# A transformer block on one core: banks for the last head pair's values, and which weight parts are made beside the attention

## The chip, the core and the metric

The kernel runs on one core of a Trainium2 chip. It uses TensorE (matrix products; PE in the profile), VectorE (DVE), ScalarE (ACT), GpSimd (POOL) and the DMA queue of SyncE (SP). The metric is the device time of one execution in microseconds (us). The times before are 2073.45, 2076.32 and 2074.26 us; their median is 2074.26 us.

## What is computed

The input x is 512 rows of 2048 numbers, all in 32-bit floats:

```python
h = rmsnorm(x, g_attn);  proj = h @ w_in            # 2048 x 6152
oa = stick_breaking_attention(8 heads);  ob = forgetting_attention(8 heads)
x = x + concat(headnorm(oa), headnorm(ob)) @ w_out  # 2048 x 2048
u = relu(rmsnorm(x, g_mlp) @ w_up);  x = x + (u * u) @ w_down
y = rmsnorm(x, g_final)
```

Every operand of a product is split into a high part (the value cast to TensorE's rounded 32-bit type) and a low part (what the cast lost), and each product is three matmuls: high by high, high by low, low by high.

## The kernel before, in words

There are four stages: the projections together with the attention, the output projection, the up projection, the down projection. This case is about the end of the first and the start of the second.

**Projections and attention.** The 16 heads are taken in eight pairs (`for n in range(0, 2 * NH, 2)`), the forgetting heads first, stick-breaking heads 6 and 7 last. For each pair `project_q` makes queries and keys of both heads (four products, `accq` in the profile), and `accumulate_v` makes the values of two pairs at a time, or, for the last pair, of that pair alone (`accv`). The weights come in 512 KB pieces through three buffers (tag `wraw`), are split by ScalarE (`wh`) and VectorE (`wl`) into three pairs of buffers (tags `wh`, `wl`), and are multiplied. `take_v` scales and splits the values (`vh` on ScalarE, `vl` on VectorE). `attend` computes the scores (`s`), turns them into weights (`w`), transposes these (`pt`), splits them (`ph`, `pl`) and multiplies them with the values (`o`; for the last head `oq`). Then the head is normalized by its mean square (the matmuls with `onesr`, lines 273 and 274) and written to `mixed`.

Sums of `accq` and `accv` are kept in four PSUM banks of one pool, `acc`, taken in turn. `s`, `pt` and `oq` share three further banks, `o` and `ssq` one.

**Weight sums beside the attention.** `sums_of_weights(m)`, called for m = 0 to 7 during the first four pairs, loads 2 MB of `w_out`, forms the sums and differences of its four blocks which the output projection needs, and writes them to DRAM (`wsums`). It also writes some operands as ready high and low parts: for product 1 both parts (`wfirst`, made in the tile `tfirst`), for products 5 and 6 the high part (`whigh`, from the tile `thi`), the low part replacing the sum itself in `wsums`. `tfirst` and `thi` take turns in one buffer, so each waits until the one before has been written out.

**Output projection.** It works by seven block products instead of eight (Winograd's form), in the order 1, 2, 6, 5, 7, 3, 4, for two halves of columns (`db`). Each product has four pieces (`out_piece(p, db, m0)`, m0 = 4, 6, 0, 2) of 12 matmuls. A piece takes its weights in one of two ways: as ready parts, two loads of 512 KB straight into a high and a low buffer; or raw, one load of 512 KB into a `wraw` buffer (named `wo`), with the split on ScalarE and VectorE. For db = 0 the products 1, 5 and 6 go by parts, 2, 7, 3 and 4 raw. The places for high and low parts are handed out in turn by `hi_lo`: three buffers, and a fourth (`wx`, in the pool `px`) as long as `more_parts` holds it, which for db = 0 begins with product 6 and ends after product 5.

The sums of products 1, 6, 7 and 4 are kept in A (`accoa`), of 2 in B (`accob`), of 5 and 3 in C (`accoc`), for db = 0. A and B, two banks each, lie where the four `acc` banks lay; C lies in the banks of the scores. The other operands are forms of `mixed` (`g_form`: a sum of blocks where needed, then a split into `G[p]`); those of product p for m0 = 2 need heads 6 and 7 and come last. After a product `take` adds its bank to a quarter of x; a finished quarter is transposed (`tr`), written to DRAM (`xd`) and, once that write has landed, squared in place (line 686).

**What sets the order.** The kernel is written with a tile layer. Its planner places the instructions on each engine's queue by its own estimates; `tc.high_priority()` and `tc.issue_after(...)` steer it. On the chip each queue runs in the order that was planned, and an instruction that waits holds up all that stand behind it on its queue. SyncE's queue is in order too: a load that waits for its buffer holds up the loads behind it.

Of the kernel before, what the change touches and what calls it, by code (L numbers as in the profile page):

```python
# [14 lines left out]
P = 128  # L15
# [20 lines left out]
def block_kernel(ctx, tc, x, g_attn, w_in, b_f, g_out_sb, g_out_fox, w_out, g_mlp, w_up, w_down, g_final, y):  # L36
# [16 lines left out]
    up_cm = tc.tile_pool(name="u", bufs=1, side="right", reuse_waits="tile")  # L53
    up = up_cm.__enter__()
    dp = ctx.enter_context(tc.tile_pool(name="dp", bufs=1, space=bass.MemoryType.DRAM))
    acc_cm = tc.tile_pool(name="acc", bufs=4, space=PSUM, reuse_waits="tile")
    acc = acc_cm.__enter__()

    lows, last_heads = [None], [None] * 5

# [83 lines left out]


    wsums = dp.tile([P, NH // 2, 4, 2, 2, NT], F32, name="wsums")
    whigh = dp.tile([P, NH // 2, 2, 2, NT], F32, name="whigh")

    wfirst = dp.tile([P, NH // 2, 2, 2, NT], F32, name="wfirst")


    A_ORDER = (1, 4, 5, 6, 2, 7, 3)
# [5 lines left out]
    with tc.tile_pool(name="att", bufs=1, side="right", reuse_waits="tile") as at:  # L158
# [15 lines left out]
        def accumulate_v(c0, m, steps, prepare=None, more=None):  # L174

            per = NT // m
            banks = [acc.tile([P, NT], F32, tag="acc", name="accv") for _ in range(2 if more is not None else TB // per)]
# [142 lines left out]
        def v_columns(h):  # L320
            return 2 * WSB + h * P if h < NH else o0 + 2 * WSB + (h - NH) * P
# [64 lines left out]
        with tc.tile_pool(name="attp", bufs=1, space=PSUM, reuse_waits="tile") as atp:  # L386

            fl = at.tile([P, TB, NH], F32, name="fl")

            chl = at.tile([P, TB, P], F32, name="chl")  # L390
            pool.memset(chl, 0.0)
            cr = at.tile([P, TB, NH], F32R, name="cr")
            cq = at.tile([P, TB, NH], F32, name="cq")
            lf = at.tile([P, TB, 2 * NH], F32R, name="lf")
            fe = at.tile([P, TB, NH], F32, name="fe")
            for t in range(TB):
                dve.scalar_tensor_tensor(fl[:, t, :], ps[t][:, 2 * P:], r1[:, t:t + 1], bf, op0=ALU.mult, op1=ALU.add)
# [12 lines left out]
            dve.tensor_tensor(cq, cq, cps[:, :, NH:], op=ALU.add)  # L410
            act.copy(cr, cq)
            dve.tensor_copy(chl[:, :, :NH], cr.bitcast(F32))
            dve.tensor_tensor(chl[:, :, NH:2 * NH], cq, cr.bitcast(F32), op=ALU.subtract)
            cT = atp.tile([P, NT], F32, tag="o", name="cT")
            for t in range(TB):
                pe.transpose(cT[:, t * P:(t + 1) * P], chl[:, t, :], ident)
            ckT = at.tile([P, NT], F32R, name="ckT")
            act.copy(ckT, cT)

            def sums_of_weights(m):  # L420

                b = mixed[:, :NH].rearrange("p (q a) n -> p q (a n)", a=2)
                sp.dma_start(b.rearrange("p (s j) c -> p s j c", s=2),
                             w_out[2 * m * P:2 * (m + 1) * P].rearrange("(s p) (j c) -> p s j c", s=2, j=2))
                b11, b12, b21, b22 = (b[:, i] for i in range(4))
                first = at.tile([P, 2, NT], F32R, tag="thi", name="tfirst")
                split(first[:, 0], first[:, 1], b11[:, :NT])
                sp.dma_start(wfirst[:, m // 2, :, m % 2], first.bitcast(F32))
                dve.tensor_tensor(b11, b12, b11, op=ALU.subtract)
                dve.tensor_tensor(b12, b22, b12, op=ALU.subtract)  # L430
                dve.tensor_tensor(b22, b22, b11, op=ALU.subtract)
                dve.tensor_tensor(b21, b21, b22, op=ALU.subtract)
                t12 = b[:, ::3, :NT]
                hi = at.tile([P, 2, NT], F32R, tag="thi", name="thi")
                act.copy(hi, t12)
                dve.tensor_tensor(t12.bitcast(F32R), t12, hi.bitcast(F32), op=ALU.subtract)
                sp.dma_start(whigh[:, m // 2, :, m % 2], hi.bitcast(F32))
                sp.dma_start(wsums[:, m // 2, :, :, m % 2], b.rearrange("p q (d c) -> p q d c", d=2))

            for n in range(0, 2 * NH, 2):  # L440
                def project(i):
                    h = order[n + i]
                    e = (o0 if h >= NH else 0) + h % NH * P
                    return project_q(e, 2 * i, rbq), project_q(e + WSB, 2 * i + 1, rb)

                def attend(i, qk):
                    h = order[n + i]
                    with tc.high_priority():
                        (attend_fox if h >= NH else attend_sb)(h % NH, v, i, *qk)

                qk = [project(0), project(1)]
                if n < NH:
                    sums_of_weights(n)
                    sums_of_weights(n + 1)

                if n == 2 * NH - 2:
                    ps = accumulate_v([v_columns(order[n])], 2 * P, [4] * 4)
                    with tc.high_priority():
                        vs = take_v(ps)
                elif n % 4 == 2:  # L460
                    c = [v_columns(order[n + i]) for i in (0, 2)]
# [6 lines left out]
    acc_cm.__exit__(None, None, None)  # L468

# [145 lines left out]
    def out_piece(p, db, m0):  # L615

        hi, lo = (w.rearrange("p (a b) -> p a b", a=2) for w in hi_lo(2 * NT))
        if db == 0 and p == 1:
            begun_ = [sp.dma_start(w.bitcast(F32), wfirst[:, m0 // 2, i]) for i, w in enumerate((hi, lo))][1]
        elif db == 0 and p in (5, 6):  # L620
            begun_ = sp.dma_start(hi.bitcast(F32), whigh[:, m0 // 2, p - 5])
            sp.dma_start(lo.bitcast(F32), wsums[:, m0 // 2, 3 * (p - 5), db])
# [70 lines left out]
    for db in range(2):  # L693
        if db == 1:
            begin(0, 0, db)
        else:
# [3 lines left out]
            with tc.issue_after(last_heads[2].ins):  # L700
                for p in (4, 5):
                    g_form(p, (4, 8), (0, 2), (2, 3))
            out_piece(1, 0, 4)
            with tc.issue_after(last_heads[3].ins):
                out_piece(1, 0, 6)
# [411 lines left out]
```

## Time and profile before

| | |
|---|---|
| median of three runs | 2074.26 us |
| profiled execution, its own time | 2072.58 us |
| span of the profile | 2070.8 us |
| TensorE busy | 2050.2 us, 99% |
| VectorE busy | 1612.9 us, 78% |
| ScalarE busy | 1049.7 us, 51% |
| moved by DMA | 400.49 MB, 193 GB/s on average |

The profile is of one execution. A row of the timeline gives the start in us from the span's start, the duration, engine, line of the kernel before, operation, output and inputs, how many equal ones were merged and, in brackets, how long the engine was idle before it and what ended that. Matmuls overlap: of a row of matmuls it is the distance from start to start that counts, not the duration. A row of stretches gives the busy time of each engine in the stretch, then the TensorE clock, the share of time in which the DMA engines were busy, and GB/s.

### The profile page before, as it was taken

What the parts mean: (1) busy time and instruction counts of PE and PEld (TensorE: products, weight loads), DVE (VectorE), ACT (ScalarE), POOL (GpSimd) and SP (SyncE); (2) the same over time, 40 slices, a digit from 0 to 9 for tenths busy, and PEclk for the clock granted to TensorE, in tenths of its full rate; (3) what the DMA queues carried; (4) which work ended last, traced back from release to release, by engine and by line L of the source; (5) the groups of instructions that cost most, each with busy time, mean ns of one, the idle gap of its engine ahead of it and who ended that gap; (6) DMA issues with size and microseconds to landing.
All of it is one profiled execution on the core that took longest, in us unless ns stands there. A gap on an engine that the chain in (4) does not pass through costs nothing.

```text
span 2070.8 us, 29864 instructions
## 1 busy us (share of the span) xinstructions
PE 2050.2 (99%) x12000; PEld 1822.9 (88%) x12000; DVE 1612.9 (78%) x1764; ACT 1049.7 (51%) x1420; POOL 55.1 (3%) x76
## 2 busy tenths in 40 slices
PE   9999999999999999999999999999999999999998
PEld 8888888888897889999999999999888888888886
DVE  6767754657568478888888888888789888989895
ACT  6434433444455466656656665665743343433434
POOL 0000000000000000000000000000000000000003
PEclk9999999999999999999999999999999999999999
DMA  7878732323336872665665666567855664763722
GB/s 252 289 273 288 240 91 73 82 81 84 79 114 245 287 264 98 204 194 178 208 197 184 204 212 193 177 211 248 296 198 214 255 238 160 281 236 140 273 93 102
DMA packets 258218, 400.49 MB, mean 193 GB/s; under 512 B 9328, under 2 KB 154784, under 8 KB 250528
## 3 DMA queue, kind: packets, MB, share of 16 engines
q1 hardware_dynamic: 257120, 396.46, 57.1%
q8 instruction: 94, 1.54, 0.3%
q10 hardware_dynamic: 960, 2.13, 0.3%
q14 instruction: 44, 0.36, 0.1%
HBM read 307.85 MB, written 90.70 MB: 192 GB/s over the span
## 4 chain that ended last, share of the span: by engine, by line
PE 94%; DVE 3%; DMA 1%; issue 1%; ACT 1%; SPq 0%; ACTq 0%
PE accd L96 7%; PE accd L97 7%; PE accd L98 7%; PE psa L97 6%; PE psa L98 6%; PE psa L96 6%; PE accq L96 6%; PE accq L98 6%; PE accq L97 6%; PE psc L98 3%; PE psc L97 3%; PE psc L96 3%; PE accv L96 3%; PE accv L97 3%; PE accv L98 3%; PE psb L96 1%
## 5 line engine op out<-in xcount | busy, mean ns | idle before, releaser
L63 ACT CAST wh<-wu 128x1024 fp32r<-128x1024 f32 x171 | 178.3, 1048 | 136.4 <-PE psa L97 57.1
L64 DVE TENSOR_TENSOR wl<-wu,wh 128x1024 fp32r<-128x1024 f32 x171 | 208.1, 1221 | 45.8 <-ACT wh L63 44.9
L98 PE MATMUL psa<-f,wl 128*128 128x256 f32 x792 | 224.2, 283 | 0.3 <-DVE wl L64 0.3
L97 PE MATMUL psa<-f,wh 128*128 128x256 f32 x792 | 224.2, 283 | 0.1
L96 PE MATMUL psa<-f,wh 128*128 128x256 f32 x792 | 224.1, 283 | 0.0
L63 ACT CAST wh<-wd 128x1024 fp32r<-128x1024 f32 (+1 forms) x135 | 133.2, 996 | 173.2 <-PE accd L98 104.5
L96 PE MATMUL accq<-hH,wh 128*128 128x512 f32 x512 | 200.5, 392 | 0.1
L98 PE MATMUL accq<-hH,wl 128*128 128x512 f32 x512 | 200.4, 391 | 0.0
L97 PE MATMUL accq<-hL,wh 128*128 128x512 f32 x512 | 200.3, 391 | 0.0
L64 DVE TENSOR_TENSOR wl<-wd,wh 128x1024 fp32r<-128x1024 f32 (+1 forms) x135 | 153.7, 1149 | 35.4 <-ACT wh L63 35.0
L63 ACT CAST wh<-wraw 128x1024 fp32r<-128x1024 f32 (+2 forms) x101 | 101.9, 1010 | 153.1 <-PE accq L97 92.9
L98 PE MATMUL accd<-wh,uf 128*128 128x512 f32 x432 | 168.1, 389 | 0.0
L97 PE MATMUL accd<-wl,uf 128*128 128x512 f32 x432 | 168.1, 389 | 0.0
L96 PE MATMUL accd<-wh,uf 128*128 128x512 f32 x432 | 167.9, 389 | 0.0
L64 DVE TENSOR_TENSOR wl<-wraw,wh 128x1024 fp32r<-128x1024 f32 (+2 forms) x101 | 119.3, 1183 | 56.3 <-ACT wh L63 49.9
L63 ACT CAST wx<-wd 128x1024 fp32r<-128x1024 f32 (+1 forms) x89 | 89.2, 1005 | 125.9 <-PE accd L98 72.1
L98 PEld LDWEIGHTS psa<-f,wl 128*128 128x128 f32 x792 | 152.0, 192 | 0.5 <-DVE wl L64 0.5
L97 PEld LDWEIGHTS psa<-f,wh 128*128 128x128 f32 x792 | 152.0, 192 | 0.4 <-DVE f L64 0.3
L96 PEld LDWEIGHTS psa<-f,wh 128*128 128x128 f32 x792 | 152.0, 192 | 0.1
L64 DVE TENSOR_TENSOR wx<-wd,wx 128x1024 fp32r<-128x1024 f32 (+1 forms) x89 | 102.6, 1161 | 23.9 <-ACT wx L63 23.7
L96 PEld LDWEIGHTS accq<-hH,wh 128*128 128x128 f32 x512 | 96.2, 188 | 19.7 <-PE accv L98 0.5
L98 PEld LDWEIGHTS accq<-hH,wl 128*128 128x128 f32 x512 | 96.1, 188 | 19.5
(338 smaller groups left out, 5558.2 us busy)
## 6 DMA issues: line engine op xcount, KB each, us to landing
wu<-in_w_up_dram SPq DMA_DIRECT2D x60, 1024.0 KB, 6.9
ufd<-st SPq DMA_DIRECT2D x98, 512.0 KB, 7.0
wd<-in_w_down_dram SPq DMA_DIRECT2D x48, 1024.0 KB, 6.3
wraw<-in_w_in_dram SPq DMA_DIRECT2D x84, 512.0 KB, 3.9
uf<-ufd SPq DMA_DIRECT2D x42, 1024.0 KB, 6.8
mixed<-in_w_out_dram SPq DMA_DIRECT2D x8, 2048.0 KB, 8.3
wsums<-mixed SPq DMA_DIRECT2D x8, 2048.0 KB, 8.1
wo<-wsums SPq DMA_DIRECT2D x24, 512.0 KB, 5.3
```

The source lines that it names most:

```text
L63: ins = act.copy(hi, src)
L64: lows[0] = dve.tensor_tensor(lo, src, hi.bitcast(F32), op=ALU.subtract)
L96: pe.matmul(out, sh, mh, start=first, stop=False, skip_group_check=True)
L97: pe.matmul(out, sh, ml, start=False, stop=False, skip_group_check=True)
L98: return pe.matmul(out, sl, mh, start=False, stop=last, skip_group_check=True)
```

## The change

1. The pool `acc` becomes two pools of two banks, `accs[0]` and `accs[1]`, taken by turns; they lie where A and B will lie. The values of the last pair are taken from `accs[1]` alone, that is, from B's two banks.
2. `sums_of_weights` writes both parts for products 1 and 2 (`wraws`, two splits of 512 columns through the tile `tboth`) and the high part for product 6 alone (512 columns). Before it was both parts for product 1, and the high parts for 5 and 6 (one cast and one difference of 1024 columns). Per call it makes three small writes (512, 512 and 256 KB) beside `wsums`; before, two (512 and 512 KB).
3. For db = 0, product 2 goes by parts, and product 5 raw.
4. The fourth place for parts, `wx`, is there from product 1 on, not from product 6.
5. `take_squares` is tied to the last cast of output weights only where there has been one.

```diff
-    acc_cm = tc.tile_pool(name="acc", bufs=4, space=PSUM, reuse_waits="tile")
-    acc = acc_cm.__enter__()
+    acc_cms = [tc.tile_pool(name=f"acc{c}", bufs=2, space=PSUM, reuse_waits="tile") for c in "ab"]
+    accs = [cm.__enter__() for cm in acc_cms]
+    acc_turn = [0]
+    class acc:
+        @staticmethod
+        def tile(*args, **kwargs):
+            acc_turn[0] += 1
+            return accs[1 - acc_turn[0] % 2].tile(*args, **kwargs)
...
-                first = at.tile([P, 2, NT], F32R, tag="thi", name="tfirst")
-                split(first[:, 0], first[:, 1], b11[:, :NT])
-                sp.dma_start(wfirst[:, m // 2, :, m % 2], first.bitcast(F32))
+                for w, raw in zip(wraws, (b11, b21)):
+                    both = at.tile([P, 2, NT], F32R, tag="thi", name="tboth")
+                    split(both[:, 0], both[:, 1], raw[:, :NT])
+                    sp.dma_start(w[:, m // 2, :, m % 2], both.bitcast(F32))
...
-                t12 = b[:, ::3, :NT]
-                hi = at.tile([P, 2, NT], F32R, tag="thi", name="thi")
-                act.copy(hi, t12)
+                t2 = b22[:, :NT]
+                hi = at.tile([P, 2, NT], F32R, tag="thi", name="thi")[:, 0]
+                act.copy(hi, t2)
...
-                    ps = accumulate_v([v_columns(order[n])], 2 * P, [4] * 4)
+                    ps = accumulate_v([v_columns(order[n])], 2 * P, [4] * 4, pool_=accs[1])
...
-        if db == 0 and p == 1:
-            begun_ = [sp.dma_start(w.bitcast(F32), wfirst[:, m0 // 2, i]) for i, w in enumerate((hi, lo))][1]
-        elif db == 0 and p in (5, 6):
+        if db == 0 and p in (1, 2):
+            begun_ = [sp.dma_start(w.bitcast(F32), wraws[p - 1][:, m0 // 2, i]) for i, w in enumerate((hi, lo))][1]
+        elif db == 0 and p == 6:
...
+            more_parts.append(lambda: parts_at(px, "px"))
             out_piece(1, 0, 4)
...
-            if db == 0 and p == 6:
-                more_parts.append(lambda: parts_at(px, "px"))
...
-                with tc.issue_after(casts[0].ins):
+                with ExitStack() as order_:
+                    if casts[0] is not None:
+                        order_.enter_context(tc.issue_after(casts[0].ins))
                     take_squares()
```

More of the change, by code (lines that the diff above doesn't have):

```diff
@@ L146, in block_kernel @@
     wsums = dp.tile([P, NH // 2, 4, 2, 2, NT], F32, name="wsums")
-    whigh = dp.tile([P, NH // 2, 2, 2, NT], F32, name="whigh")
-    wfirst = dp.tile([P, NH // 2, 2, 2, NT], F32, name="wfirst")
+    whigh = dp.tile([P, NH // 2, 2, NT], F32, name="whigh")
+    wraws = [dp.tile([P, NH // 2, 2, 2, NT], F32, name=f"wraws{p}") for p in (1, 2)]
     A_ORDER = (1, 4, 5, 6, 2, 7, 3)
@@ L172, in transpose_x, with accumulate_v @@
             return split(hH[k], hL[k], ps, g_in[:, k:k + 1])
-        def accumulate_v(c0, m, steps, prepare=None, more=None):
+        def accumulate_v(c0, m, steps, prepare=None, more=None, pool_=None):
             per = NT // m
-            banks = [acc.tile([P, NT], F32, tag="acc", name="accv") for _ in range(2 if more is not None else TB // per)]
+            banks = [(acc if pool_ is None else pool_).tile([P, NT], F32, tag="acc", name="accv")
+                     for _ in range(2 if more is not None else TB // per)]
             if more is not None:
@@ L432, in sums_of_weights @@
                 dve.tensor_tensor(b21, b21, b22, op=ALU.subtract)
-                t12 = b[:, ::3, :NT]
-                hi = at.tile([P, 2, NT], F32R, tag="thi", name="thi")
-                act.copy(hi, t12)
-                dve.tensor_tensor(t12.bitcast(F32R), t12, hi.bitcast(F32), op=ALU.subtract)
-                sp.dma_start(whigh[:, m // 2, :, m % 2], hi.bitcast(F32))
+                t2 = b22[:, :NT]
+                hi = at.tile([P, 2, NT], F32R, tag="thi", name="thi")[:, 0]
+                act.copy(hi, t2)
+                dve.tensor_tensor(t2.bitcast(F32R), t2, hi.bitcast(F32), op=ALU.subtract)
+                sp.dma_start(whigh[:, m // 2, m % 2], hi.bitcast(F32))
                 sp.dma_start(wsums[:, m // 2, :, :, m % 2], b.rearrange("p q (d c) -> p q d c", d=2))
@@ L467, in block_kernel @@
     up_cm.__exit__(None, None, None)
-    acc_cm.__exit__(None, None, None)
+    for cm in acc_cms[::-1]:
+        cm.__exit__(None, None, None)
     form2 = ctx.enter_context(tc.tile_pool(name="form2", bufs=1, reuse_waits="tile"))
@@ L617, in out_piece @@
         hi, lo = (w.rearrange("p (a b) -> p a b", a=2) for w in hi_lo(2 * NT))
-        if db == 0 and p == 1:
-            begun_ = [sp.dma_start(w.bitcast(F32), wfirst[:, m0 // 2, i]) for i, w in enumerate((hi, lo))][1]
-        elif db == 0 and p in (5, 6):
-            begun_ = sp.dma_start(hi.bitcast(F32), whigh[:, m0 // 2, p - 5])
-            sp.dma_start(lo.bitcast(F32), wsums[:, m0 // 2, 3 * (p - 5), db])
+        if db == 0 and p in (1, 2):
+            begun_ = [sp.dma_start(w.bitcast(F32), wraws[p - 1][:, m0 // 2, i]) for i, w in enumerate((hi, lo))][1]
+        elif db == 0 and p == 6:
+            begun_ = sp.dma_start(hi.bitcast(F32), whigh[:, m0 // 2])
+            sp.dma_start(lo.bitcast(F32), wsums[:, m0 // 2, 3, db])
         else:
```

## The prediction

> **What bounds the kernel now.** I read the span first, then the stretches, then TensorE's own waits, then its timeline where it waited, and last what ran on VectorE, ScalarE and the queue in front of each wait.
>
> ```profile
> span 2070.8 us, 29864 instructions
> 40.00:100.00 60.00, 60.00 (x290) 50.23 (x289) 48.10 (x76) 31.70 (x56) 1.20 (x2) 1.00 0.82 279
> ...
> 620.00:630.00 10.00, 7.63 (x55) 6.76 (x54) 7.02 (x9) 5.24 (x9) 1.02 (x3) 1.00 0.68 238
> ...
> 660.00:670.00 10.00, 9.46 (x46) 7.48 (x45) 9.01 (x12) 6.91 (x15) 0.00 (x0) 1.00 1.03 411
> 670.00:680.00 10.00, 8.34 (x35) 6.25 (x36) 4.96 (x6) 2.67 (x4) 0.00 (x0) 1.00 1.02 415
> ```
>
> TensorE bounds the kernel. In the stretches shown, and in nearly all others, it has no gap, at the full clock; it has some between 620 and 680, where the attention ends and the output projection begins. So the change can win only there, and elsewhere it can only lose.
>
> ```profile
> PE o L98 <- DVE vl L67: 1.5, 2, 1.1
> PE o L96 <- ACT vh L66: 0.9, 1, 0.9
> ...
> 614.43 0.40 PE L96 MATMUL s<-uh 128*128 128x512 f32 x1
> ...
> 625.35 0.40 PE L96 MATMUL o<-ph,vh 128*128 128x512 f32 x1
> ...
> 630.56 1.31 PE L242 MATMUL pt<-ident,w 128*128 128x128 f32 x10
> ...
> 631.77 0.44 PE L96 MATMUL accoa<-wh,g 128*128 128x512 f32 x1
> ...
> 637.50 0.39 PE L96 MATMUL oq<-ph,vh 128*128 128x512 f32 x1
> ...
> 639.36 0.44 PE L96 MATMUL accoa<-wh,g 128*128 128x512 f32 x1
> ...
> 642.37 0.39 PE L96 MATMUL accob<-wh,g 128*128 128x512 f32 x1
> ...
> 645.09 0.39 PE L273 MATMUL oq<-pl,onesr 128*128 128x512 f32 x1
> ```
>
> The reader is to see: the last values' product (`accv`) is done when `o` begins at 625.35, and TensorE waits for the split values (`vh`, `vl`). The ten transposes and the last `o` take 631.77 - 630.56 = 1.21 us. Twelve such matmuls without waits (`oq`) take 639.36 - 637.50 = 1.86, eleven about 1.74; here eleven took 630.56 - 625.35 = 5.21, so 3.5 us are lost. Twelve output matmuls take 645.09 - 642.37 = 2.72, 0.227 each.
>
> ```profile
> 656.65 0.39 PE L97 MATMUL accoa<-wl,g 128*128 128x512 f32 x1
> 657.33 0.50 PE L98 MATMUL accoa<-wh,g 128*128 128x512 f32 x1 [0.29 <-DVE g L64]
> ...
> 668.91 0.39 PE L96 MATMUL accoc<-wh,g 128*128 128x512 f32 x1
> 669.84 0.50 PE L97 MATMUL accoc<-wl,g 128*128 128x512 f32 x1 [0.54 <-DMA wl<-wsums]
> ...
> 672.24 0.39 PE L98 MATMUL accoc<-wh,g 128*128 128x512 f32 x1
> 673.76 0.50 PE L96 MATMUL accoa<-wh,g 128*128 128x512 f32 x1 [1.13 <-ACT wh L63]
> ...
> 675.02 0.50 PE L97 MATMUL accoa<-wl,g 128*128 128x512 f32 x1 [0.53 <-DVE wl L64]
> ```
>
> Four later waits, from start to start less 0.23: 0.45 (a form of head 6 or 7), 0.70 (a transfer) and 1.29 (a cast); the fourth by its idle time, 0.53 (a split). All in all 3.5 + 3.0 = 6.5 us are lost here, 0.31% of the span. That is the most this change can win in this stretch.
>
> **The change part by part.** I go by the order in which the planner put the changed kernel's instructions on each queue.
>
> *The banks.* A's banks are now free when the third projection's sums have been taken, so 24 output matmuls of product 1 (two pieces, 5.44 us) stand among and behind the twelve `o`: one, two `o`, three, one `o`, four, and so on. They cover the 3.5 us. The second bank of B is the fourth projection's, so the last values must wait for its sums to be taken.
>
> ```profile
> 601.55 0.68 DVE L212 TENSOR_TENSOR qf<-accq,rb 128x512 f32<-128x512 f32 x1
> 623.58 2.96 DVE L289 TENSOR_TENSOR_SCAN w<-w 128x256 f32<-128x256 f32 x4
> ...
> 630.47 2.15 DVE L64 TENSOR_TENSOR g<-mixed,g 128x1024 fp32r<-128x1024 f32 x3
> 632.54 2.16 DVE L516 TENSOR_TENSOR mixed<-mixed 128x1024 f32<-128x1024 f32 x3
> 634.61 1.49 DVE L64 TENSOR_TENSOR pl<-pt,ph 128x1280 fp32r<-128x1280 f32 x1
> ...
> 643.89 1.22 DVE L64 TENSOR_TENSOR wl<-wo,wh 128x1024 fp32r<-128x1024 f32 x1
> ...
> 647.07 0.69 DVE L106 SCALAR_TENSOR_TENSOR n<-n,ra 128x512 f32<-128x512 f32 x1
> ...
> 652.47 0.75 DVE L277 SCALAR_TENSOR_TENSOR mixed<-os_last,g_rest,ph 128x512 f32<-128x512 f32 x1
> ...
> 661.70 2.42 DVE L520 TENSOR_TENSOR mixed<-mixed 128x1024 f32<-128x1024 f32 x3
> 628.41 1.27 ACT L291 ACTIVATE w<-w 128x1280 f32<-128x1280 f32 x1 [2.38 <-DVE w L290]
> 629.74 0.76 POOL L234 TENSOR_SCALAR_AFFINE_SELECT w<-w 128x384 f32<-128x384 f32 x2 [6.87 <-ACT w L291]
> 667.25 0.63 ACT L686 ACTIVATE x<-x 128x512 f32<-128x512 f32 x1 [0.59 <-DMA xd<-x]
> ```
>
> They are taken by 602.2. The planner puts about 32 matmuls of the first bank in front (256 columns wide, so half of 0.227 and a little, 0.12: 3.8 us from 599.1 to 602.9), so I cost this at nothing. Should VectorE take the sums 2 us later, TensorE would lose some 1.3.
>
> The scores of the last head stand 15 matmuls earlier (15 x 0.12 = 1.8 us, from 614.43 to 612.6), and no `vl` is ahead of the scan any more. So the scan begins near 621.1, its end and the difference (1.4) follow by 625.9, the exponential (1.27) runs from 625.9 rather than 628.41, GpSimd (0.76) is done by 628.0 rather than 630.5. The transposes have their turn after twelve output matmuls and eight `o`, at 625.4 + 2.7 + 1.4 = 629.5. Two `vh` follow the exponential (627.2), each with its `vl`, some 0.47 apiece in alternation: 629.1. VectorE then has the same six form instructions as at 630.47 and 632.54 (634.61 - 630.47 = 4.14) and `pl` (1.4): 634.6, against 636.0 before. TensorE is there at 625.35 + 24 x 0.227 + 1.74 + 1.21 = 633.7. **First remaining wait: 0.9 us.**
>
> *From `pl` to the last heads' forms.* Four splits of raw weights for product 2 (`wl<-wo`, 1.22 each) leave VectorE's queue here, 4.9 us, with four casts on ScalarE. But TensorE's own order now sets the pace: the last sum of squares stands behind `oq` (1.86), 24 output matmuls (5.44) and four single ones (0.9), at 634.6 + 8.2 = 642.8. Both heads' chains then run interleaved: one scaling, two activations of each head (0.69 and 4 x 0.63, as the row at 667.25), eight VectorE steps of about 0.63 in alternation (0.69 for one alone). Head 6 is done near 649.8, head 7 near 650.5, against 653.2 before. TensorE gets to head 6's form after 30 more matmuls (6.8) at 649.8, and the cast (about 0.4) ends at 650.2. The 18 matmuls left of products 1 and 2 end at 654.3. Product 6 must wait until product 1's sums are added to x (1.2 on VectorE, behind four small forms and a large one): 654.6. **Second and third: 0.5 and 0.3 us.**
>
> *Product 5 raw.* Its four splits (4 x 1.22 on VectorE, 4 x 1.05 on ScalarE) now stand between the forms of products 7 and 3. The first two weights are loaded long ahead. The next go into the buffers these free, and the first piece of product 7 into that of x's first quarter, which is now loaded before the weights (SP's queue: x and one `wo` ahead of product 1's parts) and holds one of three raw buffers from about 604 on. Its squares wait on ScalarE behind the last forms of product 3: VectorE ends their sums (the three at 661.70, 2.42, three more like them, and 3.8 of others, behind 654.6) near 663.2; four casts follow, and the squares (twice 0.63 and a little) end near 667.8 instead of 668.6.
>
> ```profile
> wo<-wsums SPq DMA_DIRECT2D x24, 512.0 KB, 5.3
> 660.33 9.46 DMA wl<-wsums
> wfirst<-tfirst SPq DMA_DIRECT2D x8, 512.0 KB, 3.1
> L63 ACT CAST tfirst<-mixed x8: 611/620/622, 39.5 to 236.7; 128x512 fp32r<-128x512 f32 x8
> L435 ACT CAST thi<-mixed x8: 1040/1054/1057, 47.4 to 243.0; 128x1024 fp32r<-128x1024 f32 x8
> L437 SPq DMA_DIRECT2D whigh<-thi x8: 366/366/367, 48.5 to 244.1; - x8
> ```
>
> From there a load (5.3), and a cast (1.05) behind that of the piece before: 674. One matmul of product 7 stands in TensorE's queue ahead of the rest of product 5. TensorE is there at 654.6 + 48 x 0.227 + 0.9 (eight transposes) + 25 x 0.227 = 672.1. **Fourth: 1.9 us**, between nothing (landing in the 3.1 of the small writes, the squares a little earlier) and 5 (landing in 9.46).
>
> *The sums beside the attention.* Per call ScalarE casts 3 x 512 instead of 512 + 1024 columns (3 x 0.62 for 0.62 + 1.05: 0.2 us more), VectorE likewise, SP issues one more write (0.37) and 256 KB more are written; eight times. The buffer is waited for once more per call, a write's 3.1 us, on ScalarE's queue, and behind it stand casts of projection weights. TensorE hides this: it had no gap in 60 us of the very stretch, and a weight piece of 24 matmuls lasts 5.4 us. The later `wsums` writes hold up the next load of `w_out` by a few us, and no reader of these is near. I take nothing; the bounds are nothing and the price under the rivals.
>
> *The transfers.* Product 2 by parts moves 4 MB where it moved 2, product 5 the reverse: the same bytes, earlier, where DMA was busy 68% (620 to 630) and not all the time (660 to 680). The fourth place lets one more piece be under way. Cost nothing: one piece takes 1 MB in 1,048,576 / 411 = 2.55 us at the rate of the stretch 660 to 670, just under TensorE's 2.72.
>
> **The sum.** Remaining waits 0.9 + 0.5 + 0.3 + 1.9 = 3.6 us, against 6.5: 2.9 us less. From 680 on each engine has the same order as before but for a few places, so the gain is kept to the end. The profiled execution took 2072.58 us, 1.78 beside its span, and would take 2069.7. The median of the runs shown is 2074.26, 1.7 above it; so I predict 2071.4 us, 0.14% less. No change can be told from one of under 0.2% (4.1 us) here, and this is one.
>
> **The rivals.**
>
> *The gain in full.* The fourth wait falls away, or all four do: the matmul of product 7 finds its cast done when the squares are 2 us earlier or the load lands in about 3. Then 2.9 + 1.9 = 4.8 to 6.5 us are won: 2067.8 to 2069.5. For it speaks that the queue is nearly idle by then; against, that ScalarE has some 4 us of form casts ahead of the squares. 0.27.
>
> *Transfers bind.* With four places a load has three pieces' time, 8.2 us, before its piece is due. Two 512 KB loads that land in 9.46, as one did at 660.33, are 1.3 us late each time round: three rounds, 3.9 us, 2075.3. Against it: that was one load, and such loads' median is 5.3. The Trainium skill, "DMA: Bandwidth & Descriptors", section "Where 436 GB/s comes from", has a rule for the same side: transfers from HBM to SBUF are bound by HBM at about 358 GB/s per core. By it, as an estimate, a piece takes 2.93 us, 0.21 over TensorE's, 2.5 over the twelve pieces of products 1, 2 and 6, which gives 2073.9. The trace disagrees, with 411 and 415 GB/s. 0.13.
>
> *The forms or the buffers do less than that.* The waits move and stay as long in sum (head 7's chain no earlier, the cast for product 7 four us late): no gain, 2074.3. It is also the case in which the change does not do what it says. 0.10.
>
> *Slower: the third turn of one buffer.* In a call of `sums_of_weights` ScalarE now stops twice for a write to land. In the first two calls TensorE has no weights in store beyond the next piece, and if the planner put the second stop ahead of a cast that is due, TensorE waits for the write, its issue and the cast. Price 3.1 + 0.37 + 0.62 = 4.1 us per call, twice 8.2, less the gain: 2079.6. It decides from a landing above about 5.4 us, the time of one piece; the landings of that kind had a median of 3.1, which speaks against, and DMA was busy 82% of 40 to 100, which speaks for. 0.13.
>
> **How the numbers follow.** The forecast, 1.2 to 4.1 us won, has 0.37. Faster by over 0.2%: the gain in full and its edge, 0.30. Slower by over 0.2%: 0.13. Within: 0.57. The range reaches from all four waits gone, 2067.8, to 2077.0, which leaves out the slower case and little else; the likeliest alone is 2070.2 to 2073.0.
>
> **What would show it.** Right: output matmuls of product 1 among the last `o`, no wait for `vl`; busy share near 10.00 in 620 to 630; product 2's pieces without casts; a wait of the last head's product for `pl`, and one at the first matmul of product 7 for a cast whose load began when the squares ended. Wrong: any gap of TensorE's before 620; waits for `wh`, `wl` loads from `wraws`; the squares' buffer no issue; a gain given back after 740, where ScalarE waits for the quarters' writes.

## The result, and the profile after

The changed kernel takes 2069.86 us (median of 15 runs, 2068.72 to 2072.93); the kernel before, beside it, 2074.06 us (15 runs, 2072.41 to 2076.32). The ratio is 0.9981, with a 95% interval from 0.9974 to 0.9987: 0.19% less, 2.7 to 5.4 us. The profiled execution took 2070.68 us, with a span of 2069.0. That is 0.8 above its median, while the profiled execution of the kernel before was 1.5 below its own, so the two profiles differ by 1.8 us in span where the medians differ by 4.2.

The stretches of the changed kernel, columns as in the prediction, with one more from the start of the up projection:

```profile
620.00:630.00 10.00, 10.00 (x75) 9.55 (x74) 7.17 (x9) 5.17 (x9) 1.53 (x4) 1.00 0.69 241
...
660.00:670.00 10.00, 8.55 (x42) 6.94 (x41) 10.00 (x13) 8.72 (x17) 0.00 (x0) 1.00 0.87 328
670.00:680.00 10.00, 10.00 (x46) 8.29 (x45) 6.85 (x8) 3.83 (x4) 0.00 (x0) 1.00 0.71 243
...
800.00:830.00 30.00, 28.73 (x240) 28.53 (x239) 28.44 (x38) 18.50 (x31) 0.00 (x0) 1.00 0.25 81
```

TensorE is full from 620 to 630, where it was busy for 7.63 of 10 us; its gap from 670 to 680 is gone as well (8.34 before). There is a larger one between 660 and 670 (busy 8.55 us, 9.46 before). VectorE is busy all the time there, but the next view shows that TensorE waits for a transfer. Between 800 and 830 it is busy 28.73 us, for 29.56 before.

TensorE's own waits of the changed kernel between 600 and 840 us, by what they waited for (us in total, times, longest):

```profile
PE accoa L104 <- DMA wh<-whigh: 1.5, 1, 1.5
PE psa L106 <- DVE wl L72: 1.3, 1, 1.3
PE oq L104 <- DVE pl L72: 0.5, 1, 0.5
PE accoc L105 <- DVE wl L72: 0.4, 1, 0.4
PE accoa L104 <- ACT g L71: 0.4, 1, 0.4
```

The same places in its timeline, in order of time (start, us, engine, line, operation, out<-in; lines of the changed kernel are 8 to 12 higher):

```profile
627.17 0.40 PE L104 MATMUL accoa<-wh,g 128*128 128x512 f32 x1
627.41 0.39 PE L104 MATMUL o<-ph,vh 128*128 128x512 f32 x1
...
634.84 1.48 DVE L72 TENSOR_TENSOR pl<-pt,ph 128x1280 fp32r<-128x1280 f32 x1
...
635.46 0.39 PE L106 MATMUL accoa<-wx,g 128*128 128x512 f32 x1
...
636.37 0.50 PE L104 MATMUL oq<-ph,vh 128*128 128x512 f32 x1 [0.53 <-DVE pl L72]
...
651.65 0.41 ACT L71 CAST g<-mixed 128x256 fp32r<-128x256 f32 x1 [3.91 <-DVE mixed L286]
...
652.11 0.50 PE L104 MATMUL accoa<-wh,g 128*128 128x512 f32 x1 [0.38 <-ACT g L71]
...
652.34 1.42 SPq L667 DMA_DIRECT2D x<-in_x_dram  x3
...
654.78 0.70 SPq L632 DMA_DIRECT2D wh<-whigh  x1
...
662.78 0.47 PE L104 MATMUL accoc<-wh,g 128*128 128x512 f32 x1
...
664.71 0.50 PE L104 MATMUL accoa<-wh,g 128*128 128x512 f32 x1 [1.45 <-DMA wh<-whigh]
...
668.40 0.63 ACT L697 ACTIVATE x<-x 128x512 f32<-128x512 f32 x1 [0.28 <-DMA xd<-x]
...
674.02 1.05 ACT L71 CAST wh<-wo 128x1024 fp32r<-128x1024 f32 x1 [1.23 <-DMA wo<-wsums]
...
675.51 0.39 PE L104 MATMUL accoc<-wh,g 128*128 128x512 f32 x1
675.74 0.39 PE L104 MATMUL accoa<-wh,g 128*128 128x512 f32 x1
...
818.60 0.39 PE L106 MATMUL psa<-f,wl 128*128 128x256 f32 x1 [1.27 <-DVE wl L72]
```

What is to be seen: output matmuls of product 1 among the last `o`, and no wait for `vl`. From start to start, less the regular distance, TensorE loses 0.68 at `oq`, 0.54 at head 6's form, 0.05 at product 6 and 1.70 at product 6's third piece, where a high part of the weights has not landed. At the first matmul of product 7 (675.74) it loses nothing. At 818.60 it loses 1.44.

Where the 1.8 us of the two profiles come from: I count from the first `accv` (6.47 before, 7.02 after, a load of x 0.5 us later) to the first up-projection product `psb` (801.98 and 799.58), that is, 795.51 and 792.56 us, 2.95 less. The losses between 620 and 760 fell from 7.7 (the 6.5 of the prediction, by distances 6.6, and 1.06 at 757, which it did not count) to 3.5 (the 2.97 above and 0.56 at 755): 4.2 won. 1.3 of it were lost again between the first `accv` and 607 (below, under the sums), which leaves the 2.95. The later start takes 0.55 more. After 801.98 and 799.58 another 0.6 are lost in sum: 0.9 at 818, less 0.3 elsewhere.

So the two profiles account for 1.8 of the 4.2 us by which the medians differ. The rest lies in the executions that were not profiled: that of the kernel before which was profiled is faster than most, and no profile shows where its slower ones lose time.

### The profile page after: what moved, and what is told of

It is laid out like the page before. It is cut to its first block, busy times and chain, and to the rows that moved or that the text cites. A ratio compares the mean times of both kernels' runs of the same rounds, so it can differ in the third digit from the quotient of the medians.

```text
span 2069.0 us, 29903 instructions
## 1 busy us (share of the span) xinstructions
PE 2049.1 (99%) x12000; PEld 1823.1 (88%) x12000; DVE 1614.9 (78%) x1772; ACT 1048.9 (51%) x1428; POOL 55.1 (3%) x76
## 4 chain that ended last, share of the span: by engine, by line
PE 86%; DMA 6%; DVE 6%; issue 2%; ACT 1%; SPq 0%; POOL 0%; ACTq 0%; DVEq 0%
PE accd L104 7%; PE accd L105 7%; PE accd L106 7%; PE psa L106 6%; PE psa L105 6%; PE psa L104 6%; PE accq L104 4%; PE accq L105 4%; PE accq L106 4%; PE psc L106 3%; PE psc L105 3%; PE psc L104 3%; DMA wsums<-mixed 2%; DMA mixed<-in_w_out_dram 2%; PE accv L104 2%; PE accv L105 2%
## 5 line engine op out<-in xcount | busy, mean ns | idle before, releaser
L104 PE MATMUL accd<-wx,uf 128*128 128x512 f32 x288 | 112.1, 389 | 1.1 <-ACT wx L71 1.1
```

What stands on the lines that cost most here:

```text
L104: pe.matmul(out, sh, mh, start=first, stop=False, skip_group_check=True)
```

## The experiments

All times are medians; each run stands beside runs of the kernel before on the same chip. The last two columns are from each run's profile: from the first `accv` to the last transposes `pt` before 620 (what is lost during the attention), and from there to the first `psb` (what is lost at its end and in the output projection). They are of one execution each. In sums_behind and x_late_sums_behind TensorE's order is another, with more matmuls ahead of `pt`, so their two columns cannot be set beside the others.

| run | us | before | ratio, 95% | accv to pt | pt to psb |
|---|---|---|---|---|---|
| kernel before | | | | 598.73 | 196.78 |
| changed kernel | 2069.86 | 2074.06 | 0.9974 to 0.9987 | 600.01 | 192.55 |
| after_again | 2070.04 | 2073.51 | 0.9973 to 0.9991 | 598.81 | 192.50 |
| banks_alone | 2071.11 | 2073.51 | 0.9980 to 0.9998 | 598.36 | 193.98 |
| parts_alone | 2074.11 | 2073.51 | 0.9995 to 1.0012 | 600.67 | 196.94 |
| fourth_late | 2069.56 | 2073.51 | 0.9972 to 0.9990 | 599.16 | 194.84 |
| x_late | 2069.97 | 2073.73 | 0.9974 to 0.9992 | 598.99 | 192.38 |
| x_later | 2068.74 | 2073.25 | 0.9971 to 0.9988 | 599.18 | 192.26 |
| five_parts | 2071.47 | 2073.73 | 0.9980 to 0.9998 | 599.44 | 193.25 |
| parts_12 | 2074.91 | 2073.25 | 0.9999 to 1.0017 | 597.72 | 198.45 |
| sums_extra | 2070.96 | 2073.25 | 0.9979 to 0.9997 | 598.92 | 194.19 |
| sums_behind | 2084.41 | 2073.73 | 1.0037 to 1.0062 | 609.29 | 197.80 |
| x_late_sums_behind | 2081.93 | 2073.73 | 1.0026 to 1.0051 | 609.39 | 195.83 |
| x_tail | 2069.82 | 2073.51 | 0.9970 to 0.9988 | 601.37 | 192.61 |

### The changed kernel again

> The changed kernel a second time. Its first profile spans 2069.0 us, 1.8 less than the kernel before, while the medians differ by 4.2. Between 600 and 800 us the profile shows 4.2 us won (first up-projection product psb at 799.58 for 801.98, after a start 1.8 us later); it loses 0.5 at the start, about 1.3 between 180 and 600 (a wait of o for vl at 190, one of accq at 340) and 0.9 at 818 (psa waits for wl). Theory: these losses outside 600 to 800 are chance of one execution; in a second profile most are gone, and the span is near 2067.5. Rival: they belong to the change (the sums beside the attention); then the waits at 190, 340 and 818 come back at the same places. The median is near 2069.9 either way.

The wait for `whigh` (1.63), that of `oq` (0.68) and that of the form (0.54) came back at their places and sizes, and so did 1.43 at 817 and the wait of `accq` for `vl` near 340 (0.4): these belong to the change, as the rival had it. The wait of `o` for `vl` near 190 fell from 0.7 to 0.2, and the span to 2068.4, not to 2067.5: that part varies from execution to execution.

### The banks alone

```diff
-    acc_cm = tc.tile_pool(name="acc", bufs=4, ...)
+    acc_cms = [tc.tile_pool(name=f"acc{c}", bufs=2, ...) for c in "ab"]
...
+                    ps = accumulate_v(..., pool_=accs[1])
```

> The kernel before with the two pools of banks and the last values in B's banks, nothing else. Theory (the prediction's steps): the 3.5 us at o for vl are covered by product 1's matmuls, the wait of oq for pl appears with 0.9 to 2.3, since four raw splits still stand on VectorE, and the later waits for a form, a transfer, a cast and a split stay at 3.1: 1.2 to 2.6 us won, 2071.5 to 2072.9. Rival: the banks are worth nothing without the parts, because pl and the last heads' chains are as late as before: 2073.5 to 2074.5. Second rival: the banks carry the whole gain: 2070.

2.4 us less, inside the forecast of 1.2 to 2.6. Its waits between 600 and 840 us:

```profile
PE ssq L281 <- ACT n L71: 1.4, 1, 1.4
...
PE accoc L104 <- DMA wx<-whigh: 0.7, 1, 0.7
...
PE accoc L105 <- DMA wx<-wsums: 0.4, 1, 0.4
PE accoc L104 <- DMA wh<-whigh: 0.3, 1, 0.3
```

The 3.5 us at `o` are covered. A wait of 1.4 for `n`, which a head's sum of squares needs, takes the place that I gave to `pl`. The later waits do not stay as they were: product 5's parts wait 2.0 by distances for transfers, for 0.70 in the kernel before, and the waits for a cast and a split at product 7 are gone.

### The parts alone

```diff
-    acc_cms = [...]; accs = [...]        # and pool_=accs[1]
+    acc_cm = tc.tile_pool(name="acc", bufs=4, ...)
```

> The changed kernel with the one pool of four banks as before: parts of products 1, 2 and 6 and the early fourth place stay. Theory: TensorE again waits some 3.5 us at o for vh and vl; of the later waits the form's 0.5 and the transfer's 1.7 stay as in the changed kernel, and the cast's wait at product 7 is hidden behind the transfer's: about 1 us won, 2072.5 to 2073.5. Rival: the parts carry the gain (VectorE and ScalarE, free of four splits, hand on vl earlier): 2070 to 2071. Second rival: without the banks the parts only cost (sums beside the attention): 2074.5 or more.

No gain: 2074.11 beside 2073.51. That is above the forecast of 2072.5 to 2073.5 and below the second rival's 2074.5. The profiled execution, 2075.84, is the slowest of the eleven. Its waits:

```profile
PE accoa L96 <- DMA wh<-whigh: 1.6, 1, 1.6
PE o L98 <- DVE vl L67: 1.5, 2, 1.1
```

The wait for the last values stands as before, and the stretch before 606 us is 1.9 us longer than in the kernel before. So the parts earn nothing without the banks: banks alone 2.4, parts alone nothing, both 3.5 to 4.2. What the parts add to the banks, 1.1 us between the medians of banks_alone and after_again, is not certain: the two intervals overlap.

### The fourth place late

```diff
-            more_parts.append(lambda: parts_at(px, "px"))   # ahead of product 1
...
+            if db == 0 and p == 6:
+                more_parts.append(lambda: parts_at(px, "px"))
```

> The changed kernel with the fourth place for parts from product 6 on, as before. Theory (the prediction's transfers at cost nothing): three places give a load two pieces' time, 5.4 us, and pairs of parts land in about 4 to 5: nothing to 1 us lost, 2069.9 to 2071, with small waits of accoa or accob for a load from wraws. Rival (transfers bind in this stretch): each round of three comes late by 1 to 2 us, 3 to 5 us lost: 2073 to 2075.

2069.56: no loss that can be measured. In its profile one load from `wraws` is late. The profiled execution, 2071.43, is the slowest of the eleven, and loses time after that wait also to a lower clock, which the section on the hardware shows:

```profile
PE accob L104 <- DMA wh<-wraws: 1.9, 1, 1.9
...
PE accoa L104 <- ACT wh L71: 0.8, 1, 0.8
```

The second row is the fourth wait of the prediction, the first matmul of product 7 waiting for its cast: where nothing holds TensorE up at product 6's third piece, it is there.

### x's quarters behind the parts of product 6

```diff
-                if db == 0 and p == 6 and m0 == 6:
+                if db == 0 and p == 6 and m0 == 2:
                     ... begin(0, 1, db)
-                if db == 0 and p == 5 and m0 == 4:
+                if db == 0 and p == 5 and m0 == 0:
                     ... begin(1, 1, db)
...
             if p == 3:
-                begin(1, 0, db)
+                ...
+                    if db == 0:
+                        later_.enter_context(tc.issue_after(ins.ins))
+                    begin(1, 0, db)
```

> The changed kernel with the loads of x's other three quarters moved behind the parts of product 6 on SyncE's queue (two of them behind its last piece, one to product 3). In the changed kernel these three loads, 1.5 MB, stand at 652.3 us ahead of the parts of product 6's third piece, whose high part lands 9.88 us after its issue while the DMA engines are busy all the time; TensorE loses 1.6 to 1.7 us there, in both profiles. Theory: the wait is the queue's order, and goes; the wait for the cast of product 7's first weight, which it hid, comes up with nothing to 1.0 us (0.96 in the run with the late fourth place): 0.7 to 1.7 us won, 2068.3 to 2069.4. Rival: the load is late because its buffer comes free late; it lands as late without the x loads, and the time stays at 2070. Second rival: a quarter of x now comes too late for its sum, and VectorE holds up what stands behind it: over 2071.

The wait for `whigh` is gone: the loads of x ahead of it on the queue were its cause. In its place stands the wait for the cast, 1.39 by distances. The chain of waits of this run, in order of time (start, us, what):

```profile
656.96 8.75 DMA xd<-x
...
665.74 1.35 ACT x L697 x4
...
667.10 3.53 DMA wo<-wsums
...
671.67 1.15 DVE wl L72
...
672.86 1.05 ACT wh L71
...
673.95 0.50 PE accoa L104
```

Up to the squares this is the chain of the prediction's fourth wait: x's first quarter is written out, then squared, which frees its buffer. From there the view goes by the piece before, whose load is the one at 667.10, and by VectorE. Product 7's own load was issued behind that one, at 667.53, and took 5.2 us, so that it landed just before the cast at 672.86. VectorE's split of the piece before ended at the same time. Which of the two the cast waited for, the next run tells.

The median did not move: one wait was exchanged for the other, 0.3 us smaller. It lies above the forecast of 2068.3 to 2069.4.

### One load of x further back

```diff
-                if db == 0 and p == 5 and m0 == 4:
-                    with tc.issue_after(ins.ins):
-                        begin(1, 1, db)
...
+                ins = out_piece(7, 0, 4)
+                with tc.issue_after(ins.ins):
+                    begin(1, 1, db)
```

> The run with the late x loads, with one load moved further: x's quarter for products 5 and 7 behind the raw load of product 7's first piece; TensorE's, VectorE's and ScalarE's orders are the same. In that run TensorE loses 1.39 us at product 7 for the cast of a piece whose load could only begin when the squares had ended (667.1) and then stood in the queue behind this load of x (512 KB, 1.25 us at 420 GB/s) and another weight. Theory: the load's end is what counts, and the wait falls to nothing to 0.4 us; about 1 us won against the run before it: 2068.5 to 2069.3 in the median, span of the profile 2066 to 2066.5. Rival: the cast is held up by something else (VectorE's split of the piece before ends just then, 672.7), and the wait stays at 1.2 to 1.5: 2069.5 to 2070.

The wait at product 7 fell from 1.39 to 0.3 us by distances, with VectorE's and ScalarE's orders unchanged, and the cast (672.26) no longer comes behind that split: the load's end was what counted. But 0.9 came back at 754 (a wait of `accoc` for `wl`, 1.45 for 0.55, behind a load of `wo` that took 5.93 us), so the stretch after the transposes is hardly shorter. The profile of x_tail, which has this edit too, shows the same wait, 1.47, and 0.7 at product 7. The median, 2068.74, is the lowest of all runs; but its interval overlaps with that of the changed kernel, the profile does not show where it would be won, and I do not call it faster.

### Product 5 by parts too, and product 6 raw

> The changed kernel with product 5 by parts too (products 1, 2, 6 and 5 by parts; the high part of 5 made beside the attention as in the kernel before). No raw load is then needed before product 7. Theory: between 650 and 670 us the transfers bind, and 2 MB more at the 328 GB/s of 660 to 670 take 6.4 us, of which the 10.9 us of product 5's matmuls hide some: waits of accoc for loads of high and low parts of 1 to 3 us in sum beside the 1.7 at product 6, and no wait for the cast of product 7: 2070.5 to 2073. Rival (what binds there is VectorE and ScalarE, which lose four splits): the time falls by up to 1 us, to 2069.

> The changed kernel with product 6 raw: parts for products 1 and 2 alone, no high part made for product 6, so that the buffer in the sums has two turns as in the kernel before, and 2 MB less are moved between 645 and 665 us. Theory: transfers no longer bind there (no wait for whigh), and the sums cost as before the change (0.5 to 1.6 us back), but four splits more, 4.9 us, stand on VectorE between 645 and 668, which is busy 91 to 100% from 650 on; they push the forms of products 7 and 3 and the raw splits of 5 back, and TensorE waits 2 to 5 us for wl or g: 2070.5 to 2074. Rival: VectorE's gaps of 640 to 650 take them up, and the time falls: 2068 to 2069.5.

With products 1, 2, 6 and 5 by parts: 2071.47, inside the forecast. There is no wait at product 7, and none at product 6 either, where the forecast kept 1.7, but three for the parts of product 5, 1.9 us by distances, while the DMA engines are busy all the time:

```profile
PE accoc L104 <- DMA wx<-whigh: 0.7, 1, 0.7
...
PE accoc L105 <- DMA wx<-wsums: 0.3, 1, 0.3
```

With product 6 raw (its high part is not made): 2074.91, above the forecast of at most 2074, and no wait for a transfer. The forms and splits are late instead, and behind the second of these waits the clock falls, which adds some 1.6 us (last section):

```profile
PE accoa L104 <- ACT g L71: 2.6, 1, 2.6
PE accoc L105 <- DVE wx L72: 2.3, 1, 2.3
```

So the choice is measured on both sides: with two products by parts VectorE is late, and the time is 5 us longer than with three. With four the transfers are late; there the 1.5 us more are not certain, for the intervals overlap.

### The sums beside the attention

```diff
+                extra = at.tile([P, 2, NT], F32R, tag="thi", name="textra")
+                split(extra[:, 0], extra[:, 1], b21[:, :NT])
+                sp.dma_start(wextra[:, m // 2, :, m % 2], extra.bitcast(F32))
```

> The kernel with the banks alone (2071.11 us, first accv to the transposes near 605 us: 598.36 us), and in each call of the weight sums one more split of 512 columns through the same buffer and one more write of 512 KB, which nobody reads: the price of the sums by itself. The result's operands are unchanged. The prediction priced this at nothing, with a bound of 8.2 us if TensorE waits for weights in the first two calls. Theory: a longer sum on VectorE's queue delays the values' low parts behind it near 190 us, and the stretch before 605 us grows by 0.5 to 1.6 us: 2071.6 to 2072.7. Rival: no cost, and the 0.45 to 1.65 us seen with the new sums are other things: 2071.1. Second rival: the third turn of the buffer also holds up weights before 70 us: 2073 or more.

```diff
-                if n < NH:
+                if n < NH and n % 4 != 2:
...                                           # behind take_v:
+                    if n < NH:
+                        with tc.issue_after(last_heads[2].ins):
                             sums_of_weights(n)
                             sums_of_weights(n + 1)
```

> The changed kernel with the calls of the weight sums for pairs 1 and 3 planned behind the split of the values in the same pair. In the profiles with the new sums o waits near 190 us for vl, which stands on VectorE behind the sums' differences (0.2, 0.6 and 1.2 us in three of four), and accq near 340 for vl (0.4); the distance from the first accv to the transposes of 606 us is 0.45 to 1.65 us longer than with the old sums. Theory: the sums' place on VectorE's queue is the cause; both waits go, and 0.5 to 1.4 us are won: 2068.5 to 2069.5. Rival: the loss is the writes and loads on SyncE's queue, and comes back at another place: 2070. Second rival: the sums, later by some us, run into the following pair and cost more: 2071 or above.

> Both edits of the two runs above together. Theory: they lie 450 us apart and add up: 1.2 to 3 us won against the changed kernel, 2067 to 2068.8. Rival: as for each alone, 2070.

The extra split alone, on the kernel with the banks alone: 2070.96 for 2071.11, no difference in the time. In the profile the attention's stretch is 0.56 us longer, and the stretch after 800 us, where the planner's order fell out otherwise, 0.5 shorter (0.3 of waiting near 818 for 1.3). This run does not price the sums of the changed kernel, though: in its order the first difference near 190 us begins at 190.98, behind the `vl`, and no `o` waits for one. With the sums made for four products it is the same (190.87).

What the sums do in the changed kernel is seen near 190 us. First the row of the kernel before for the first difference, then the changed kernel:

```profile
178.86 1.22 DVE L429 TENSOR_TENSOR mixed<-mixed 128x1024 f32<-128x1024 f32 x1
```

```profile
182.54 1.23 DVE L439 TENSOR_TENSOR mixed<-mixed 128x1024 f32<-128x1024 f32 x1
...
185.09 1.22 DVE L440 TENSOR_TENSOR mixed<-mixed 128x1024 f32<-128x1024 f32 x1
...
187.35 0.48 DVE L75 SCALAR_TENSOR_TENSOR vl<-accv,r1v,vh 128x256 fp32r<-128x256 f32 x1
...
189.48 1.66 DVE L75 SCALAR_TENSOR_TENSOR vl<-accv,r1v,vh 128x256 fp32r<-128x256 f32 x4
...
190.01 0.45 PE L106 MATMUL o<-ph,vl 128*128 128x384 f32 x1 [0.71 <-DVE vl L75]
```

The differences of the sums (`mixed`) stand ahead of `vl` on VectorE, in both kernels, and they wait for the load of `w_out`, which waits for the write of the sums before. In the changed kernel the call before has one turn of the buffer more, and its last write is issued 6.1 us later; the load (173.37 for 169.12) and the first difference (182.54 for 178.86) follow later too. That write in the kernel before and in the changed one:

```profile
160.44 0.37 SPq L438 DMA_DIRECT2D wsums<-mixed  x1
```

```profile
166.50 0.37 SPq L448 DMA_DIRECT2D wsums<-mixed  x1
```

SyncE's waits for such writes, first of the kernel before and then of the changed one, over 0 to 300 us:

```profile
SPq L423 <- DMA wsums<-mixed: 23.2, 7, 4.7
```

```profile
SPq L432 <- DMA wsums<-mixed: 34.7, 7, 7.0
```

Over the runs with the sums and the order of the changed kernel, the first of those differences began between 181.0 and 183.6 us, and the wait of `o` for `vl` was nothing when it began at 181.0, 0.2 at 181.4, 0.6 at 181.5, 0.7 at 182.5, 1.2 at 182.9 and 1.3 at 183.6. The attention's stretch goes with it, but for some tenths: 598.8 to 601.4.

Planning two pairs' sums behind the values took the wait at 190 away, but not the one near 340, which grew from 0.4 to 1.6, and the time rose by 12 and 14.5 us against x_late and the changed kernel, which lack this edit. Its largest waits:

```profile
PE pt L251 <- POOL w L243: 7.6, 1, 7.6
PE o L106 <- DVE vl L75: 2.6, 1, 2.6
```

An edit at 190 us moved the planner's order at 615: the last head's scores now stand at 622.60 instead of 614.46, and TensorE has nothing left to do when its transposes wait for the mask. So this run says nothing about the price of the sums; both edits together (2081.93) showed the same. That the added split is what makes the sums late in the changed kernel rests on the order of the call and the rows above; no run tests it alone in that order.

### The start of the up projection

```diff
+                    if q == 7:
+                        if j == 1:
+                            left_form(q, 1, 1)
+                            left_form(q, 1, 0)
-                    if (q, j) != (6, 0):
+                    elif (q, j) != (6, 0):
                         left_form(q, 1, 1 - j)
```

> The run before (x's loads behind product 7's first weight) with one edit more, at the start of the up projection: the two halves of the form for product 7 are planned behind the weight split of the second unit's product 6. In the profile of the kernel before TensorE waits 0.34 us for wl near 820; in the changed kernel, and in every run whose VectorE queue has a form (0.6 us) more ahead of that split, 1.27. Theory: this 0.9 us, which the changed kernel gives back after 740, is the planner's order on VectorE alone; with a sum of the form and its split (1.2 us) moved behind, the wait falls to under 0.4, and 0.7 to 1.1 us are won: 2067.6 to 2068.1. Rival: VectorE is full there (28.4 of 30 us from 800 to 830), and the wait comes back at product 7 for its form: 2068.7 or more.

The rival held: the wait for `wl` (1.44) went, and one of 1.00 for the form came 5 us later; 2069.82. VectorE is full there. That the kernel before, five_parts, sums_extra and sums_behind lose 0.5 at this place and the others 1.4 is the order of one form (0.6 us) against one split; it is shown by the orders, not by this run.

## Why the prediction was right or wrong, point by point

**The total.** Forecast 2.9 us less, 2071.4 us; measured 4.2 (2.7 to 5.4), 2069.86. The forecast gain lies inside the interval, but this is partly luck. Several terms of the sum were off and partly cancelled. The sum was for the profiled execution, 2069.7, and that one took 2070.68; the median was then put 1.7 above it, as in the kernel before, and lies 0.8 below it. The forecast also held that a change of under 0.2% cannot be told here; with 15 runs of each the interval leaves out no change.

**The banks: right.** The 3.5 us at `o` were covered, the first `accoa` stands ahead of the first `o`, and no wait appeared near 600 for the fourth projection's sums. The run with the banks alone earned 2.4 of the 4.2 us.

**First to third wait: right in place, near in size.** Forecast 0.9, 0.5 and 0.3; measured 0.68, 0.54 and 0.05. Everything stands some 1.8 us later than forecast, because the attention ended later; within that, head 6's form was ready when forecast (651.65 and 0.41 against 649.8 and 0.4).

**Fourth wait: the mechanism right, the sum wrong.** In the changed kernel it does not show: a transfer holds TensorE up for 1.70 us at 664.71, 11 us earlier, and the cast at 674.02 is done 0.67 us before TensorE is there; its load took 4.2 us, for 5.3 in the sum. Taking the transfer's wait away brought the cast's out, 1.39 (forecast 1.9), through the forecast chain; moving a load of x away from ahead of it brought it down to 0.3. The two waits lie behind one another on the same engine, so the larger counts, not both.

**"The transfers ... Cost nothing": wrong.** The chain of waits of the changed kernel has this one row for it, start and us:

```profile
654.78 9.88 DMA wh<-whigh
```

I priced the transfers by the rate of a stretch, and dismissed a landing of 9.46 us because "such loads' median is 5.3". That median was of raw loads over the whole kernel. The issues of the kernel before between 598 and 690 us (KB each, median us to landing) have the right rows:

```profile
wl<-wsums SPq DMA_DIRECT2D x6, 512.0 KB, 9.7
wh<-whigh SPq DMA_DIRECT2D x6, 512.0 KB, 8.8
```

For the parts of products 5 and 6, the loads that count here, 9 us was the usual landing in that stretch. The rival "transfers bind" had the mechanism right, with 3.9 us where 1.70 came; its place was one load behind three loads of x, not three rounds.

The rule of the Trainium skill, "DMA: Bandwidth & Descriptors", section "Where 436 GB/s comes from", under which HBM binds at about 358 GB/s, is not what bound here: the run with four products by parts moved 409 GB/s from 665 to 675 us.

**"No reader of these is near. I take nothing": wrong.** The reader of that load is VectorE's difference ahead of `vl`. In the profiled execution TensorE loses 0.9 near 190 for it by distances. It loses 0.5 more near 340, where no difference stands just ahead of the `vl` on VectorE and the cause is open. The stretch up to `pt` is 1.3 us longer than in the kernel before, and 0.1 to 2.6 longer in the other profiles with this order. What it costs in the median is not measured. The slower rival named ScalarE's turns of the buffer in the first two calls as the place: there was no wait before 100 us, and its price of 8.2 did not come.

**"The same order as before but for a few places, so the gain is kept": wrong by 0.9 us.** One of the few places is the form ahead of a split on VectorE at 815, where VectorE is full. Against that, 0.5 was won at 755, also not forecast.

## What to carry to other kernels

Waits in a row on one engine do not add up: price the chain of each to the point where the engine needs it, and take the later, for the one that is removed may only uncover the next. For a landing time, read the issues of the very stretch and what stands ahead in the queue, not a median over the kernel. Ahead of calling moved work hidden, list what stands behind it on its engine's queue, and when its input can come: here up to 1.3 us of TensorE's waiting at one place went with the time at which one load could begin, and that changed from execution to execution.

## What the runs showed of the hardware

After some waits TensorE's granted clock fell to half. In the run with the fourth place late, after the gap from 649.5 to 651.46 (the columns are those of the stretches above):

```profile
650.00:652.00 2.00, 0.54 (x2) 0.49 (x3) 1.86 (x5) 1.61 (x4) 0.00 (x0) 0.99 1.02 373
652.00:654.00 2.00, 2.00 (x6) 1.53 (x5) 1.65 (x2) 1.28 (x3) 0.00 (x0) 0.50 0.91 216
```

Seven matmuls came 0.43 us apart instead of 0.23, and an eighth 0.38, so a wait of 1.92 us cost some 1.6 more. In the run with product 6 raw the same followed a wait of 2.26 (granted clock 0.50 from 676 to 678), but not one of 2.65 in the same execution. The Trainium skill, "TensorE: Matmul & The Clock Gate", section "Why this matters for your kernels", says that a gap of over some 3 us brings the half clock back; here shorter ones did, and not each time. No such dip stands in the profile of the changed kernel. With waits of about 2 us the clock can nearly double their price, as in these two runs.
